# A hybrid decoder step on one Trainium2 core: seven products in the MLP's middle down projections, weight sums made by DMA, six raw weight buffers

## The chip, the cores and the metric

The kernel runs on one core of one Trainium2 chip. The metric is the device time of one execution in microseconds (us). The core's engines are PE (TensorE, matmuls), DVE (VectorE), ACT (ScalarE), POOL (GpSimd) and SP (SyncE, which here only issues DMAs). A matmul reads its operands from the on-chip memory SBUF and writes to PSUM; the inputs, the outputs and the weights lie in DRAM.

## The reference

One decoder layer in fp32 for 576 token columns: 512 prompt tokens and 64 sample tokens (8 sequences of 8). Cut to what matters here:

```python
m, s_gla_new, s_ret_new = mixer_block(rmsnorm(x, g_pre_mix), pos, s_gla, s_ret, w_in, ...)
x = x + rmsnorm(m, g_post_mix)
x = x + rmsnorm(cross_attn(rmsnorm(x, g_pre_xa), mem_k, mem_v, w_xq, w_xo), g_post_xa)
hf = rmsnorm(x, g_pre_ffn)
x = x + rmsnorm(jnp.square(jax.nn.relu(hf @ w_up)) @ w_down, g_post_ffn)
```

`mixer_block` projects to a gated linear attention branch and a retention branch of 4 heads each, with one state matrix a head, and merges them. `cross_attn` has 4 heads over 256 memory tokens; the prompt's keys and values are computed from `mem`, the samples' come from caches (`cache_mem_k`, `cache_mem_v`). `w_up` is 1024 x 4096 and `w_down` 4096 x 1024. The outputs are `y`, the new states and the prompt's new memory keys and values.

## The kernel before

Activations lie transposed: 1024 features as 8 blocks of 128 partitions, and 576 columns of tokens in two halves of 288 (`NH`). Every product is made from three matmuls in the reduced fp32r format: each operand is split into a high part (a cast on ACT, L93) and the rest (a subtraction on DVE, L94), and high x high, low x high and high x low are summed in PSUM (`mm3` L250, `gemm` L255). So a product of one 128x1024 weight tile with all columns is 8 x 3 x 2 = 48 matmuls of 128x288.

**Weights.** A list `plan` holds every weight tile in the order of its use. `wfetch` (L174) issues the next load on SP into one of `N_RAW` buffers `wraw` (4 of 128x1024 in the kernel before); `wsplit` (L183) casts the oldest into `wh` (ACT) and `wl` (DVE), three of each; `wnext` (L237) hands out a split tile and keeps `N_RAW - 1` loads asked for. The samples' cached keys and values (`in_ktc`, `in_vc`) go through the same `wraw` buffers in cross attention, and are used there without a split; how many stand after each weight tile is written in `KV_AFTER` (L31).

**Stages**, in order of time: the memory's keys and values (to about 62 us); the mixers, 8 units of one branch and one head each, `UNITS` (to about 565 us); the mix projection; cross attention, in two halves with `w_xq` and `w_xo`; the MLP. A tile scheduler sets each engine's order from the program; an engine takes its instructions in that order, and a DMA queue its loads.

**MLP.** Hidden features are taken in four groups of 1024, `g` = 0 to 3. Each group has an up stage (into `hh`, `hl`, after relu and square) and a down stage that adds to `y3`. Group 0's stages and all down stages are plain: 8 tiles of 48 matmuls. The up stages of groups 1 to 3 use `sevenfold` (L273): the weight is cut into 2x2 blocks, the activations into 2x2 (features by column halves), and the four result blocks come from seven products of block sums in place of eight. A call makes two blocks of 128 features, 7 x 12 = 84 matmuls; a stage is four calls. The sums of the activations are made once (`sums_f` L656, into `fsh`, `fsl`; "S1" to "S4" name the products of sums, "A11", "A12", "A22" those of plain blocks). The sums of the weights are made on DVE, four subtractions of 128x512 a call (`minus` L213, called by `begin` L203), from two tiles of `w_ups`.

**Mixers.** For each head, DVE and POOL make the norms of the output (`mv`, then `rs` on POOL, L874, then `on` on DVE, L878 and L880), POOL makes `ks` (L1063), masks `sm` (L965), the rotary products `t` (L890) and gates `G` (L1127); `s0` is a head's state, loaded by SP.

Of the kernel before, what the change touches and what calls it, by code (L numbers as in the profile page):

```python
# [22 lines left out]
N_RAW = 4  # L23
# [3 lines left out]


RING, STAY, RAW, SEVEN = 0, 1, 2, 3
# [29 lines left out]
def decoder_step(ctx, tc, xT, memT, ktc, vc, s_gla, s_ret, w_in, w_ga, w_a2, w_mix, w_xq, w_xk, w_xv, w_xo,  # L59
                 w_up, w_ups, w_down, vecs, cst, gam, y_out, mk_out, mv_out, sg_p, sr_p, sg_s, sr_s):  # L60
# [102 lines left out]
    def seven(w, b0):  # L163
        return [(w[b0 + b][:, kh], SEVEN) for b in range(4) for kh in range(2)]
# [6 lines left out]
    wq = []  # L171
    units = []

    def wfetch():  # L174
        if plan and sum(m == SEVEN for _, m in raws) < 2:
            src, mode = plan.pop(0), RING
            if isinstance(src, tuple):
                src, mode = src
            raw = wp.tile([P, 1024], F32, name="wraw", bufs=N_RAW)
            nc.sync.dma_start(out=raw if len(src.shape) == 2 else raw.rearrange("p (k n) -> p k n", n=src.shape[2]), in_=src)  # L180
            raws.append((raw, mode))

    def wsplit():  # L183
        if units:
            units.pop(0)()
        elif raws:
            if raws[0][1] == SEVEN:
                begin()
                return
# [4 lines left out]
            pool = staying[-1] if mode == STAY else wp  # L194
            wh = pool.tile([P, 1024], F32R, name="wh")
            wl = pool.tile([P, 1024], F32R, name="wl")
            split(wh, wl, raw)
            ready.append((wh, wl))

    def halves(w):  # L200
        return w.rearrange("p (q n) -> p q n", q=2)

    def begin():  # L203


        while len(raws) < 2:
            wfetch()
        p0, p1 = (raws.pop(0)[0] for _ in range(2))
        t = wp.tile([P, 1024], F32, name="wraw", bufs=N_RAW)
        q0, q1, qt = halves(p0), halves(p1), halves(t)  # L210

        def minus(out, a, b):
            nc.vector.tensor_tensor(out=out, in0=a, in1=b, op=ALU.subtract)  # L213

        def ring(raw):
            wh = wp.tile([P, 1024], F32R, name="wh")
            wl = wp.tile([P, 1024], F32R, name="wl")
            split(wh, wl, raw)
            ready.append((wh, wl))

        def own(raw, o, n):
            w = wq[0][:, o:o + n], wq[0][:, o + n:o + 2 * n]
            split(*w, raw)
            ready.append(w)

        def unit_a():
            ring(p0)
            wfetch()

        units.extend([unit_a, lambda: ring(t), lambda: own(p1, 0, 1024),  # L230
                      lambda: minus(q1[:, 0], q1[:, 0], qt[:, 0]), lambda: own(q1[:, 0], 2048, 512)])
        minus(qt[:, 1], q1[:, 1], q0[:, 1])
        minus(q0[:, 1], q0[:, 1], q0[:, 0])
        minus(qt[:, 0], q1[:, 1], q0[:, 1])
        wfetch()

    def wnext(n=P):  # L237

        while sum(len(r) == 2 for r in ready) < 2 and (raws or plan):
            while not units and plan and len(raws) + sum(len(r) == 1 for r in ready) < N_RAW - 1:  # L240
                n0 = len(raws)
                wfetch()
                if len(raws) == n0:
                    break
            if not raws and not units:
                break
# [24 lines left out]


    def sevenfold(x, p1, p5, u2, c11, c22, c12, c21):  # L273


# [9 lines left out]
        def more():  # L285
            if units:
                wsplit()

        while len(ready) < 3:
            wsplit()  # L290
        acc, b, c = atile()[:, :NH], otile()[:, :NH], gtile()[:, 0, :NH]
        wa, wc, wb = (ready.pop(0) for _ in range(3))
        prod(acc, wa, 0, "A11", True)
        p1(acc)
        while units:
            wsplit()
        wd = ready.pop(0)
        prod(c, wa, 1, "S1", True)
        p5(c)
        if raws and raws[0][1] == SEVEN:  # L300
            begin()
        prod(acc, wc, 0, "S2", False)
        wsplit()
        u2(acc)
        prod(b, wb, 0, "A12", True)
        more()
        c11(b)
        prod(acc, wc, 1, "S3", False)
        c22(acc)
        prod(c, wb, 1, "S4", False)  # L310
        c12(c)
        more()
        prod(acc, wd, 0, "A22", False)
        more()
        c21(acc)
# [332 lines left out]
    xnp = ctx.enter_context(tc.tile_pool(name="xnp", bufs=2))  # L648
# [4 lines left out]
    def add(out, a, b, op=ALU.add):  # L653
        nc.vector.tensor_tensor(out=out, in0=a, in1=b, op=op)  # L654

    def sums_f():  # L656

        for j in range(4):
# [5 lines left out]
            add(c2[:, 1], c2[:, 0], c2[:, 1])  # L664
            add(c2[:, 0], c1[:, 0], c2[:, 0], ALU.subtract)
            add(c1[:, 0], c2[:, 1], c1[:, 0], ALU.subtract)
            add(c1[:, 1], c1[:, 1], c1[:, 0], ALU.subtract)
            yield
            split(fsh[:, 2:4, j], fsl[:, 2:4, j], c2)
            split(fsh[:, 0:2, j], fsl[:, 0:2, j], c1)  # L670
            yield

    FQ = {"A11": (fh, fl, 0), "A12": (fh, fl, 1), "A22": (fh, fl, 3),
# [748 lines left out]
```

## Time and profile before

| | |
|---|---|
| median of 3 runs | 1206.34 us (1204.42 to 1206.52) |
| profiled execution, its own time | 1206.06 us |
| its span, first to last instruction | 1204.3 us |
| mean granted clock of PE | 0.988 of full speed |
| PE busy | 1172.6 us, 97% |
| DVE, ACT, POOL busy | 745.9, 564.3, 152.8 us |
| DMA | 158.37 MB, mean 131 GB/s |

The profiled execution took 1.8 us more than its span (start and end of the program) and 0.28 us less than the median. The engines are in step with PE almost everywhere, so what counts is the time in which PE does nothing, how many matmuls it has, and which of its two clock levels it is given. "x" in the rows counts instructions; a wait is put down to the one releaser that came last.

### The profile page before, as it was taken

To read this page: it belongs to the slowest core of one execution; us is meant where nothing else is said; L and a number is where in the kernel's file an instruction comes from. 1 tells how busy PE (TensorE), PEld (TensorE's weight loads), DVE (VectorE), ACT (ScalarE), POOL (GpSimd) and SP (SyncE) were. 2 spreads that over 40 slices of the span, in tenths; PEclk is the share of its full clock that TensorE was granted. 3 is DMA by queue.
4 is the path that set the end of the run, shared out by engine and by line. 5 is a ranking of instruction groups with operands and counts; after the bars stand their busy time and mean duration, and the time that the engine had idled before them with its cause. 6 is when DMAs were issued, how large, how long until landed. Compare 5 with 4: busy or idle time off the path is not lost.

```text
span 1204.3 us, 21958 instructions
## 1 busy us (share of the span) xinstructions
PE 1172.6 (97%) x9006; PEld 1140.8 (95%) x9006; DVE 745.9 (62%) x1332; ACT 564.3 (47%) x992; POOL 152.8 (13%) x165
## 2 busy tenths in 40 slices
PE   8999999999999999999999999999999999999995
PEld 7999999999999999999999877989999999999995
DVE  6756556565756575658677544686847457555665
ACT  6624455533544344434565444556437316415652
POOL 0621213131312231221001000000000000000000
PEclk9999999999999999999999999999999999999998
DMA  7852324242324242422644676654322322422641
GB/s 268 277 195 90 125 70 130 79 136 80 127 80 127 88 128 71 142 75 91 213 150 138 232 252 233 196 160 127 105 71 87 107 70 65 129 71 70 199 145 60
DMA packets 65621, 158.37 MB, mean 131 GB/s; under 512 B 5648, under 2 KB 34448, under 8 KB 65392
## 3 DMA queue, kind: packets, MB, share of 16 engines
q1 hardware_dynamic: 65520, 156.96, 40.9%
q8 instruction: 71, 1.16, 0.4%
q14 instruction: 30, 0.25, 0.1%
HBM read 140.68 MB, written 16.25 MB: 130 GB/s over the span
## 4 chain that ended last, share of the span: by engine, by line
PE 86%; DVE 6%; DMA 3%; ACT 3%; issue 1%; POOL 1%; SPq 0%; POOLq 0%; DVEq 0%; ACTq 0%
PE psg L252 23%; PE psg L251 23%; PE psg L253 23%; PE psa L281 4%; PE psg L281 2%; PE psa L251 1%; DVE wl L94 1%; PE psa L252 1%; PE psa L253 1%; PE pso L281 1%; DMA wraw<-in_w_xo 1%; PE pso L1241 1%; DMA wraw<-in_w_down 1%; PE psa L1084 1%; ACT wh L93 1%; DVE res L526 1%
## 5 line engine op out<-in xcount | busy, mean ns | idle before, releaser
L251 PE MATMUL psg<-xh,wh 128*128 128x288 f32 x1296 | 386.6, 298 | 3.2 <-ACT wh L93 3.2
L252 PE MATMUL psg<-xh,wl 128*128 128x288 f32 x1296 | 383.6, 296 | 2.5 <-DVE wl L94 2.5
L253 PE MATMUL psg<-xl,wh 128*128 128x288 f32 x1296 | 383.1, 296 | 0.0
L94 DVE TENSOR_TENSOR wl<-wraw,wh 128x1024 fp32r<-128x1024 f32 x197 | 243.8, 1238 | 89.9 <-ACT wh L93 88.9
L93 ACT CAST wh<-wraw 128x1024 fp32r<-128x1024 f32 x197 | 206.9, 1051 | 164.5 <-PE psg L253 104.6
L251 PEld LDWEIGHTS psg<-xh,wh 128*128 128x128 f32 x1296 | 244.3, 189 | 5.5 <-ACT wh L93 4.1
L252 PEld LDWEIGHTS psg<-xh,wl 128*128 128x128 f32 x1296 | 244.6, 189 | 3.3 <-DVE wl L94 3.2
L253 PEld LDWEIGHTS psg<-xl,wh 128*128 128x128 f32 x1296 | 244.4, 189 | 0.1
L251 PE MATMUL psg<-hh,wh 128*128 128x288 f32 x512 | 151.9, 297 | 0.7 <-DVE y L760 0.6
L252 PE MATMUL psg<-hh,wl 128*128 128x288 f32 x512 | 150.7, 295 | 0.3 <-DVE wl L94 0.3
L253 PE MATMUL psg<-hl,wh 128*128 128x288 f32 x512 | 150.7, 295 | 0.0
L251 PEld LDWEIGHTS psg<-hh,wh 128*128 128x128 f32 x512 | 96.1, 188 | 1.6 <-issue 1.1
L252 PEld LDWEIGHTS psg<-hh,wl 128*128 128x128 f32 x512 | 96.1, 188 | 0.6 <-DVE wl L94 0.6
L253 PEld LDWEIGHTS psg<-hl,wh 128*128 128x128 f32 x512 | 96.1, 188 | 0.0
L333 POOL TENSOR_TENSOR rs<-ms,mhalf 96x3 f32<-96x3 f32 (+1 forms) x11 | 11.0, 1000 | 527.4 <-DVE ms L326 527.4
L942 ACT COPY vt<-psg 128x512 f32<-128x512 f32 x16 | 9.4, 586 | 78.2 <-PE psg L253 78.2
L874 POOL TENSOR_TENSOR rs<-mv,mhalf 128x1 f32<-128x1 f32 x48 | 29.8, 621 | 112.6 <-DVE mv L869 64.5
L654 DVE TENSOR_TENSOR y<-psg,y 128x576 f32<-128x576 f32 x16 | 12.1, 758 | 50.4 <-PE psg L253 50.4
L944 DVE COPY vd<-psg 128x128 f32<-128x128 f32 x32 | 7.8, 286 | 56.0 <-ACT vt L942 56.0
L251 PE MATMUL psg<-bh,wh 128*128 128x288 f32 x128 | 38.9, 304 | 1.6 <-ACT wh L93 1.1
L252 PE MATMUL psg<-fh,wl 128*128 128x288 f32 x128 | 38.8, 303 | 0.9 <-DVE wl L94 0.9
L251 PE MATMUL psg<-fh,wh 128*128 128x288 f32 x128 | 39.0, 305 | 0.3 <-ACT fh L93 0.2
(324 smaller groups left out, 2400.2 us busy)
## 6 DMA issues: line engine op xcount, KB each, us to landing
wraw<-in_w_in SPq DMA_DIRECT2D x64, 512.0 KB, 3.6
wraw<-in_w_down SPq DMA_DIRECT2D x38, 512.0 KB, 3.7
wraw<-in_w_ups SPq DMA_DIRECT2D x24, 512.0 KB, 3.7
wraw<-in_ktc SPq DMA_DIRECT2D x16, 512.0 KB, 4.4
wraw<-in_vc SPq DMA_DIRECT2D x16, 512.0 KB, 5.2
wraw<-in_w_xq SPq DMA_DIRECT2D x14, 512.0 KB, 4.5
wraw<-in_w_xo SPq DMA_DIRECT2D x14, 512.0 KB, 5.2
wraw<-in_w_up SPq DMA_DIRECT2D x14, 512.0 KB, 4.5
```

The costliest lines, as they stand in the source:

```text
L93: nc.scalar.copy(hi, src)
L94: nc.vector.tensor_tensor(out=lo, in0=src, in1=f32(hi), op=ALU.subtract)
L251: nc.tensor.matmul(out, ah, bh, start=first, stop=False)
L252: nc.tensor.matmul(out, al, bh, start=False, stop=False)
L253: nc.tensor.matmul(out, ah, bl, start=False, stop=last)
L281: nc.tensor.matmul(out, s[:, q, k], m[:, k], start=first and k == i == 0, stop=k == 3 and i == 2, skip_group_check=True)
L333: nc.gpsimd.tensor_tensor(out=rs[:t, :n], in0=ms, in1=mhalf[:t, :n], op=ALU.pow)
L526: nc.vector.tensor_tensor(out=res[:, kk, c], in0=y[:, kk], in1=rj, op=ALU.add)
L654: nc.vector.tensor_tensor(out=out, in0=a, in1=b, op=op)
L874: nc.gpsimd.tensor_tensor(out=rs[:t], in0=mv[:t], in1=mhalf[:t, 0:1], op=ALU.pow)
L1084: nc.tensor.matmul(U[:, j * 256:(j + 1) * 256], kst[g][:, 2 * bp + j, :], vst[g], start=True, stop=True)
L1241: nc.tensor.matmul(acc[rows, :256], x(h), w[:, h], start=first, stop=last, skip_group_check=True, tile_position=(0, 32 * h))
```

## The change

The diff does four things.

1. The down stages of groups 1 and 2 use `sevenfold` too (`xh7` gives it the blocks). For that, the up stages of these groups end by making the sums of their results (`pairs`, into `hh` and `hl`) beside the plain blocks (`ha`, and the third quarter of `fh`, `fl`). Group 3's stages keep their forms. `sevenfold` evicts its own products now, and with `late` it makes the product A12 second.
2. All weight sums, of 20 calls, are made in DRAM (`t_sev`) by DMAs that `sums()` issues during the mixers, four times a unit: for each pair of calls four copies on SP (L197 after) and four transfers on POOL that add to what lies there (L195 after). The DVE subtractions of weights go. A call then loads seven pieces of 256 KB in seven DMAs, in place of two tiles of 512 KB.
3. `N_RAW` is 6 instead of 4, for all weights and the cached keys and values.
4. The weights' buffers are filled by `wmore` inside `sevenfold`; the last, half-size tile of a call has its own buffer (`LAST`, pool `wdp`).

The core of it:

```diff
-N_RAW = 4
+N_RAW = 6
...
+SUMS_AT = (2, 4, 6, 8, 10, 12, 15, 17, 19, 21)
+SUM_STEPS = (0, 0, 2, 2, 4, 6, 8, 10)
...
+    def seven(b0):
+        out = []
+        for n in range(b0, b0 + 4):
+            g, i = n // 2, n % 2
+            b = [w_sev[q, n] for q in range(4)]
+            t1, t2, t4 = t_sev[g]
+            out += [((b[0], t1[i]), RING), ((t2[0, i], t2[1, i]), RING), ((b[2], b[3]), RING), ((t4[i],), LAST)]
+        return out
...
-        plan += seven(w_ups, 4 * (g - 1))
-        plan += whole(w_down, 4 * g) + (rest(whole(w_down, 12), 0) if g == 3 else [])
+        plan += seven(8 * (g - 1))
+        plan += seven(8 * g - 4) if g < 3 else whole(w_down, 4) + rest(whole(w_down, 4), 0)
...
+    steps = {}
+    for g, at in enumerate(SUMS_AT):
+        b11, b12, b21, b22 = (w_sev[q, 2 * g:2 * g + 2] for q in range(4))
+        t1, t2, t4 = t_sev[g]
+        for n, (dst, src, plus) in zip(SUM_STEPS, (
+                (t1, b11, 0), (t2[1], b12, 0), (t1, b12, 1), (t2[1], b22, 1),
+                (t2[0], t1, 0), (t2[0], b22, 1), (t4, t2[0], 0), (t4, b21, 1))):
+            steps.setdefault(at + n, []).append((dst, src, plus))
+    clock = [0]
+
+    def sums():
+        for dst, src, plus in steps.pop(clock[0], ()):
+            if plus:
+                nc.gpsimd.dma_start(out=dst, in_=src, accum_op=ALU.add, max_dma_last_dim=8192)
+            else:
+                nc.sync.dma_start(out=dst, in_=src)
+        clock[0] += 1
...
         prod(acc, wa, 0, "A11", True)
-        p1(acc)
-        while units:
-            wsplit()
+        nc.scalar.copy(c1[:, 0], acc)
+        if late:
+            c11()
+        prod(c, wa, 1, "S1", True)
+        nc.scalar.copy(c2[:, 1], c)
+        wmore()
         wd = ready.pop(0)
...
+    def pairs(c1, c2, sh, sl):
+        add(c2[:, 1], c2[:, 0], c2[:, 1], ALU.subtract)
+        add(c2[:, 0], c1[:, 0], c2[:, 0], ALU.subtract)
+        split(sh[:, 2:4], sl[:, 2:4], c2)
+        add(c1[:, 0], c2[:, 1], c1[:, 0], ALU.subtract)
+        add(c1[:, 1], c1[:, 1], c1[:, 0])
+        split(sh[:, 0:2], sl[:, 0:2], c1)
...
+            def done1():
+                relu2(c1)
+                split(*((hh[:, 0:2, b], hl[:, 0:2, b]) if plain else (ha[:, 0, :, b], ha[:, 1, :, b])), c1)
+
+            def done21(ps):
+                relu2(c2[:, 0], ps)
+                if plain:
+                    split(hh[:, 2:4, b], hl[:, 2:4, b], c2)
+                else:
+                    pairs(c1, c2, hh[:, :, b], hl[:, :, b])
...
+        for b in range(4):
+            c1, c2 = (hp.tile([P, 2, NH], F32, name="hr") for _ in range(2))
+            y = [y3[:, 2 * b:2 * b + 2, hc(half)] for half in range(2)]
...
+            sevenfold(xh7, c1, c2, lambda: add(y[0], y[0], c1), lambda: None, done21, b == 0)
```

**Where the order of instructions moves.** Numbers behind names count buffers; "waits" names the counters that an instruction waits for (`PE_49` is PE's, `DMASW` those of POOL's transfers, `DMAHW` those of SP's).

SP in cross attention's first half, before: cached values (`in_vc`) between the tiles of `w_xq`.

```order
L180 DMA wraw_8576<-in_vc 128x1024 [waits DMAHW1_49,PE_49]
L180 DMA wraw_8607<-in_w_xq 128x1024 [waits DMAHW3_49,DVE_49]
L180 DMA wraw_8613<-in_vc 128x1024 [waits DMAHW4_49,PE_49]
L180 DMA wraw_8634<-in_vc 128x1024 [waits DMAHW7_49,DVE_49]
L180 DMA wraw_8655<-in_vc 128x1024 [waits DMAHW5_49,PE_49]
L180 DMA wraw_8687<-in_w_xq 128x1024 [waits DMAHW6_49,PE_49]
```

And with the change, at the same place:

```order
L213 DMA wraw_8654<-in_vc 128x1024 [waits DMAHW2_49,DVE_49]
L213 DMA wraw_8656<-in_vc 128x1024 [waits DMAHW7_49,PE_49]
L213 DMA wraw_8658<-in_w_xq 128x1024 [waits DMAHW3_49,DVE_49]
L213 DMA wraw_8660<-in_vc 128x1024 [waits DMAHW0_49,PE_49]
L213 DMA wraw_8691<-in_vc 128x1024 [waits DMAHW1_49,PE_49]
L213 DMA wraw_8697<-in_vc 128x1024 [waits DMAHW7_49,DVE_49]
L213 DMA wraw_8718<-in_w_xq 128x1024 [waits DMAHW4_49,PE_49]
```

The last row is the same `w_xq` tile in both. Before, its buffer is that of the fourth load ahead of it, and the load just ahead of it takes the buffer of the first row shown. With the change its buffer is that of the sixth load ahead of it, the first row shown.

PE where the up stage of group 1 hands over to its down stage, with the change (`ha` holds the plain blocks of the up stage's result, `hh` the sums; `psa`, `pso`, `psg` are the products A11, A12 and S1):

```order
L276 MATMUL pso_11464<-ha_10886,wh_11435 128x288 x2
L276 MATMUL pso_11464<-ha_10886,wl_11436 128x288
L276 MATMUL pso_11464<-ha_10886,wh_11435 128x288
L276 MATMUL psa_11463<-ha_10886,wh_11374 128x288 [waits Activation_49]
L276 MATMUL psa_11463<-ha_10886,wl_11375 128x288
L276 MATMUL pso_11464<-ha_10886,wh_11435 128x288
L276 MATMUL pso_11464<-ha_10886,wl_11436 128x288
L276 MATMUL psg_11465<-hh_10884,wh_11374 128x288
L276 MATMUL psg_11465<-hh_10884,wl_11375 128x288
L276 MATMUL psg_11465<-hl_10885,wh_11374 128x288
L276 MATMUL psg_11465<-hh_10884,wh_11374 128x288
L276 MATMUL psa_11463<-ha_10886,wh_11374 128x288 [waits DVE_49]
```

Products of plain blocks (`ha`) of the down stage stand ahead of and between those of sums (`hh`, `hl`); before, the down stage is plain, and there are no products of sums.

POOL in the mixers' third unit, before (`ql`, `ks` operands of the heads, `sm` masks):

```order
L98 TENSOR_TENSOR ql_2573<-qf_2571,qh_2572 128x512 [waits Activation_49]
L965 AFFINE_SELECT sm_2795<-sm_2795 128x128 [waits Activation_49]
L1063 TENSOR_TENSOR ks_2826<-klo_2821,cm_828 128x512 [waits DVE_49]
L965 AFFINE_SELECT sm_2860<-sm_2860 128x128 [waits Activation_49,Pool_49]
L1063 TENSOR_TENSOR ks_2890<-klo_2885,cm_828 128x512 [waits DVE_49,PE_49]
L965 AFFINE_SELECT sm_2952<-sm_2952 128x128 [waits Activation_49,Pool_49]
```

And with the change, with transfers that add into `t_sev` (its number is the pair of calls and the piece):

```order
L101 TENSOR_TENSOR ql_2588<-qf_2586,qh_2587 128x512 [waits Activation_49]
L195 DMA t_sev30<-in_w_sev 64x2048 [waits DMAHW6_49,DMASW0_49]
L986 AFFINE_SELECT sm_2816<-sm_2816 128x128 [waits Activation_49]
L1084 TENSOR_TENSOR ks_2847<-klo_2842,cm_832 128x512 [waits DVE_49]
L195 DMA t_sev31<-in_w_sev 64x2048 [waits DMAHW7_49,DMASW1_49]
L986 AFFINE_SELECT sm_2881<-sm_2881 128x128 [waits Activation_49,Pool_49]
L1084 TENSOR_TENSOR ks_2911<-klo_2906,cm_832 128x512 [waits DVE_49,PE_49]
L986 AFFINE_SELECT sm_2973<-sm_2973 128x128 [waits Activation_49]
```

Two transfers now stand between the operations, each behind a copy on SP; in all there are 40, and nine of them stand directly ahead of an `rs` operation.

SP in the same unit, with the change:

```order
L1097 DMA s0_2991<-in_s_gla 128x4x256 [waits DMAHW4_49,PE_49]
L197 DMA t_sev02<-t_sev01 16x8192 [waits DMAHW5_49,DMASW4_49]
L1116 DMA out_sgs<-sn_3000 128x2x256 [waits DMAHW6_49,DVE_49,Activation_49]
L1116 DMA out_sgs<-sn_3083 128x2x256 [waits DMAHW7_49,DVE_49,Activation_49]
L197 DMA t_sev21<-t_sev20 16x8192 [waits DMAHW0_49,DMASW5_49]
L197 DMA t_sev40<-in_w_sev 16x8192 [waits DMAHW1_49]
L197 DMA t_sev41<-in_w_sev 16x8192 [waits DMAHW2_49]
L213 DMA wraw_3095<-in_w_in 128x1024 [waits DMAHW3_49]
L1097 DMA s0_3158<-in_s_gla 128x4x256 [waits DMAHW4_49,PE_49]
```

The second state load (`s0`) stands behind four copies of 512 KB and two stores of states; before, there are no copies.

## Rows read from the trace of the kernel before

**Rows 1.** The page's list of busy engines: us, share of span, instructions.

```profile
PE 1172.6 (97%) x9006; PEld 1140.8 (95%) x9006; DVE 745.9 (62%) x1332; ACT 564.3 (47%) x992; POOL 152.8 (13%) x165
```

**Rows 2.** Busy time by stretches: mixers, cross attention, its half clock, up stage of group 1.

```profile
core 0: us, PE busy (x) PEld busy (x) DVE busy (x) ACT busy (x) POOL busy (x), PEclk, DMA share, GB/s
...
60.00:545.00 485.00, 484.25 (x3782) 475.09 (x3782) 295.80 (x669) 210.06 (x418) 110.00 (x113) 1.00 0.35 109
...
680.00:760.00 80.00, 73.82 (x626) 63.35 (x625) 33.52 (x59) 31.64 (x64) 3.07 (x6) 0.96 0.70 229
...
695.00:700.00 5.00, 5.00 (x35) 4.60 (x38) 1.14 (x1) 1.05 (x1) 0.00 (x0) 0.72 0.61 228
...
896.00:942.00 46.00, 45.56 (x340) 45.09 (x339) 31.41 (x42) 29.71 (x50) 0.00 (x0) 1.00 0.34 106
```

**Rows 3.** Waits of PE in the whole run: us, times, longest.

```profile
PE psg L252 <- DVE wl L94: 5.2, 8, 0.9
...
PE psg L251 <- ACT wh L93: 4.2, 3, 1.6
...
PE psa L281 <- ACT hr L726: 1.0, 3, 0.4
...
PE psa L956 <- ACT T L995: 0.8, 1, 0.8
```

**Rows 4.** Waits of PE from 680 to 760 us (cross attention).

```profile
PE psg L251 <- ACT wh L93: 3.2, 2, 1.6
...
PE psg L252 <- DVE wl L94: 1.7, 2, 0.9
```

**Rows 5.** The chain of waits from 684 us: start, us, what.

```profile
685.90 6.36 DMA wraw<-in_w_xq
...
694.69 0.61 PE psg L252
...
697.70 0.24 PE psg L251
```

**Rows 6.** The chain of waits in the up stage of group 1.

```profile
898.45 1.60 PE psg L281 x12
```

**Rows 7.** SP's timeline from 683 us: start, us, instruction.

```profile
682.99 2.82 SPq L180 DMA_DIRECT2D wraw<-in_vc  x3
```

**Rows 8.** ACT's groups by shape, 885 to 932 us (three sevenfold calls).

```profile
L93 ACT CAST wh<-wraw 128x1024 fp32r<-128x1024 f32 x9 | 9.5, 1055 | 2.5 <-DMA wraw<-in_w_down 2.2
...
L93 ACT CAST hh<-hr 128x576 fp32r<-128x576 f32 x4 | 2.5, 666 | 0.0
...
L717 ACT ACTIVATE hr<-hr 128x576 f32<-128x576 f32 x3 | 2.0, 683 | 0.4 <-DVE hr L654 0.4
...
L713 ACT ACTIVATE hr<-hr 128x288 f32<-128x288 f32 x3 | 1.3, 443 | 5.4 <-DVE hr L654 5.4
```

**Rows 9.** DVE's groups by shape in the same stretch.

```profile
L94 DVE TENSOR_TENSOR wl<-wraw,wh 128x1024 fp32r<-128x1024 f32 x9 | 11.0, 1224 | 15.2 <-ACT wh L93 15.2
...
L213 DVE TENSOR_TENSOR wraw<-wraw 128x512 f32<-128x512 f32 x11 | 7.6, 691 | 0.3
...
L94 DVE TENSOR_TENSOR hl<-hr,hh 128x576 fp32r<-128x576 f32 x4 | 2.8, 752 | 0.0
...
L654 DVE TENSOR_TENSOR hr<-pso,hr 128x288 f32<-128x288 f32 x3 | 1.4, 453 | 0.6 <-PE pso L281 0.6
```

**Rows 10.** POOL's groups by shape, whole run.

```profile
L1127 POOL TENSOR_TENSOR G<-G,t 128x576 f32<-128x576 f32 x14 | 20.2, 1440 | 20.0 <-ACT t L1126 20.0
...
L890 POOL TENSOR_TENSOR t<-t,t 128x576 f32<-128x576 f32 x8 | 19.2, 2398 | 35.4 <-DVE t L889 35.4
...
L1063 POOL TENSOR_TENSOR ks<-klo,cm 128x512 fp32r<-128x512 f32 x16 | 16.7, 1042 | 84.2 <-DVE klo L1040 84.2
...
L965 POOL TENSOR_SCALAR_AFFINE_SELECT sm<-sm 128x128 f32<-128x128 f32 x16 | 4.8, 298 | 95.0 <-ACT sm L964 95.0
```

**Rows 11.** Waits of DVE from 60 to 562 us.

```profile
DVE on L880 <- POOL rs L874: 13.2, 24, 0.7
```

More of the change, by code (lines that the diff above doesn't have):

```diff
@@ L170, in decoder_step @@
+    clock = [0]
[6 more added lines that the diff above has]
+        clock[0] += 1
     raws, ready, staying = [], [], []
-    wq = []
-    units = []
+    wdp = []
     def wfetch():
-        if plan and sum(m == SEVEN for _, m in raws) < 2:
+        if plan:
             src, mode = plan.pop(0), RING
-            if isinstance(src, tuple):
+            if isinstance(src, tuple) and isinstance(src[1], int):
@@ L193, in wsplit, with wmore @@
                 return
[L194 to L197, printed above, removed]
+            n = 512 if mode == LAST else 1024
+            pool = wdp[0] if mode == LAST else staying[-1] if mode == STAY else wp
+            wh = pool.tile([P, n], F32R, name="wh")
+            wl = pool.tile([P, n], F32R, name="wl")
+            split(wh, wl, raw[:, :n])
             ready.append((wh, wl))
[L200 to L206, printed above, removed]
+    def wmore():
+        while plan and len(raws) < N_RAW - 1:
             wfetch()
[L208 to L235, printed above, removed]
+        wsplit()
     def wnext(n=P):
         while sum(len(r) == 2 for r in ready) < 2 and (raws or plan):
-            while not units and plan and len(raws) + sum(len(r) == 1 for r in ready) < N_RAW - 1:
-                n0 = len(raws)
+            while plan and len(raws) + sum(len(r) == 1 for r in ready) < N_RAW - 1:
                 wfetch()
-                if len(raws) == n0:
-                    break
-            if not raws and not units:
+            if not raws:
                 break
@@ L663, in sums_f @@
             yield
[L664 to L667, printed above, removed]
+            pairs(c1, c2, fsh[:, :, j], fsl[:, :, j])
             yield
[L669 to L673, printed above, removed]
-          "S2": (fsh, fsl, 0), "S4": (fsh, fsl, 1), "S3": (fsh, fsl, 2), "S1": (fsh, fsl, 3)}
+    SQ = {"S2": 0, "S4": 1, "S3": 2, "S1": 3}
     def xf7(n):
-        h, l, q = FQ[n]
-        return h[:, q], l[:, q]
+        return (fsh[:, SQ[n]], fsl[:, SQ[n]]) if n in SQ else tuple(
+            t[:, {"A11": 0, "A12": 1, "A22": 3}[n]] for t in (fh, fl))
     y3 = None
@@ L683, in decoder_step, with xh7 @@
         hl = acta.tile([P, 4, 4, NH], F32R, name="hl", tag="xl")
+        plain = g in (0, 3)
+        ha = None if plain else biga.tile([P, 2, 2, 4, NH], F32R, name="ha", tag="biga")
+        def xh7(n):
+            if n in SQ:
+                return hh[:, SQ[n]], hl[:, SQ[n]]
+            return (fh[:, 2], fl[:, 2]) if n == "A22" else (ha[:, 0, n == "A12"], ha[:, 1, n == "A12"])
         if g == 0:
@@ L703, in decoder_step @@
                     lows.pop(0)()
+            xns.close()
+            wdp.append(ctx.enter_context(tc.tile_pool(name="wdp", bufs=1)))
             y3 = bigb.tile([P, KT, NT], F32, name="y3", tag="res")
             side.append(sums_f())
[L706 to L727 removed]
@@ L739, in decoder_step, with done21 @@
+        if plain:
+            break
+        for b in range(4):
+            c1, c2 = (hp.tile([P, 2, NH], F32, name="hr") for _ in range(2))
+            y = [y3[:, 2 * b:2 * b + 2, hc(half)] for half in range(2)]
+            def done21(ps):
+                nc.scalar.copy(c2[:, 0], ps)
+                add(y[1], y[1], c2)
+            sevenfold(xh7, c1, c2, lambda: add(y[0], y[0], c1), lambda: None, done21, b == 0)
     res2 = fsp.tile([P, KT, NT], F32, name="res2", tag="fsh")
@@ L1122, in unit @@
                 tick()
+            sums()
             for m in range(2):
@@ L1128, in unit @@
                 tick()
+            sums()
             def finish():
```

119 lines of the change are left out of this document (53 added, 66 removed).

## The prediction

> **What bounds the kernel now.** I read the page's list of busy engines first. PE is busy for 1172.6 us of the 1204.3 us span, 97% [rows 1]; the next engine, DVE, is at 62%. So the only large thing that a change can buy is fewer matmuls, and the only other thing is the 32 us in which PE stands still, and what it then loses at half its clock.
>
> The table by stretches [rows 2] says where that is. From 60 to 545 us (the mixers) PE is busy for 484.25 of 485 us. From 680 to 760 us (cross attention) it is busy for 73.82 of 80, at a mean granted clock of 0.96. In the up stage of the MLP's group 1, the first by seven products (896 to 942 us), it is busy for 45.56 of 46.
>
> PE's waits [rows 3] then name what it waited for. In the whole run the weights' casts cost it 5.2 + 4.2 = 9.4 us, the last values of an up stage (`hr` of L726) 1.0 us in three waits, and the mixers one wait of 0.8 us. In cross attention alone [rows 4] the casts cost 3.2 + 1.7 = 4.9 us, two waits on each of ACT and DVE, so two stalls of 2.45 us.
>
> The chain of waits shows what is behind the first of them [rows 5]: the load of a `w_xq` tile was issued at 685.90 us and took 6.36 us, then cast and remainder, and then 12 single matmuls from 694.69 to 697.94 us (the first and the last stand there), against 1.60 us for 12 in the MLP, 0.133 each [rows 6]. The granted clock from 695 to 700 us was 0.72 [rows 2]: after the idle stretch the chip gave the lower of its two levels (1.2 GHz) for a while. SP's row [rows 7] shows three cached value tiles going out at 682.99 us and ending at 685.81, just before that load: the `w_xq` load stood behind them in SP's order.
>
> **The change, part by part.**
>
> *The products.* Two down groups drop from 8 x 48 = 384 to 4 x 84 = 336 matmuls, together 96 fewer. At 1.60/12 = 0.133 us [rows 6] that is **-12.8 us**, and all of it is on the path, as PE is.
>
> *The two stalls of cross attention.* With four raw buffers the late `w_xq` tile takes the slot of the tile four places back, behind another load that waits for PE. With six it takes that of the sixth back, a value tile that PE has read by 682.99 us, when the loads that now reuse it go out [rows 7]: 2.9 us before 685.90, with fewer transfers ahead of it. A stall is 2.45 us, so that covers it. Each stall also cost the half clock, 3.25 us for 12 matmuls in place of 1.60, so 1.65. Together 2 x (2.45 + 1.65): **-8.2 us**. If the loads are bound by the memory (229 GB/s from 680 to 760 us [rows 2]) more buffers don't help, and this term is 0. The other 4.5 us of casts that PE waits for lie elsewhere; I leave them, and half of them, 2.3 us, go into the range's lower end.
>
> *DVE's sums of weights.* 48 instructions of 0.691 us [rows 9], 33 us, go from DVE. They stand beside matmuls: 0.
>
> *The up stages of groups 1 and 2.* Here work is added: the eight calls now also make the sums of the activations. Per call, ACT has three casts of 1.055, one of at most 0.666, eight operations on 288 columns of 0.443, two on 576 of 0.683 and three casts of 576 of 0.666 [rows 8]; with every one in sequence 3.2 + 0.7 + 3.5 + 1.4 + 2.0 = 10.8 us. DVE has three remainders of 1.224, four of 0.752, and eight operations on 288 columns of 0.453 [rows 9]: 10.3 us. A call's 84 matmuls take 84 x 0.133 = 11.2 us. So both fit, with 0.4 and 0.9 us to spare: **0**. If they don't, a call waits for one cast, 1.055, and eight of them cost 8.4 us.
>
> *Handing over.* Where an up stage ends, PE waits for the last `hr` values, 1.0 us in three waits now [rows 3]. Five stages now begin or end with products by sums. In two of them the chain behind the last product is longer by two subtractions (2 x 0.453) and a split (0.666 [rows 8] + 0.752 [rows 9]), 2.3 us in all; but the change's order runs A11 and A12 of the down stage first, which need only the older values, and these are 2 x 1.60 us of cover. So I take 0.3 us for each of the five, the size of one of the three waits: **+1.5 us**. The bounds are 0 and 2 x 2.3 + 3 x 1.0 = 7.6.
>
> *The mixers.* They get 40 copies (SP) and 40 accumulating transfers (POOL) of 512 KB. That is 80 x 0.524 MB = 42 MB in 485 us, 86 GB/s on top of 109 at a DMA share of 0.35 [rows 2]; in proportion the share becomes 0.63, or 0.91 if each byte is moved twice. From 680 to 760 us the share was 0.70 at 229 GB/s, so there is room for the first; weights are asked for several tiles of 48 x 0.133 = 6.4 us ahead. On SP, a state load now stands behind up to four copies: 5 x 0.524/229 = 11.4 us, while its reader comes some 270 matmuls, 36 us, later. Both 0.
>
> POOL is the open one, because no accumulating transfer is in the trace of before. From below, POOL's short `sm` operation is 0.30 us; from above, its long `t` operation 2.40 [rows 10]. I take 1.04, that of `ks`, a value between the two: the accumulate hands a transfer on and computes nothing, but names many more pieces than a copy of one tile. Nine of the 40 stand directly ahead of an `rs` operation, for which DVE then waits (24 waits of at most 0.7 us at one such line [rows 11]): 9.4 us on DVE. DVE is busy for 295.8 of 485 us [rows 2], and PE had one wait in the mixers [rows 3]; a fifth of it reaching PE is **+2 us**. The bounds are 0 and 40 x 2.40 = 96.
>
> By the Trainium skill (SBUF — State Buffer, "SBUF: two separate sides") a transfer that POOL issues has its descriptors written by GpSimd, which is locked out while DVE runs certain two-port operations; it tells of one that took about 3100 ns in place of 620. That speaks against this change, since DVE is busy for 61% of the mixers; the trace of before has no transfer from POOL in them, but POOL's own 128x576 operations read 1.44 us at one line and 2.40 at another [rows 10]. By the Trainium skill's two figures 40 x 2.5 = 100 us could be lost, if PE waited for every one.
>
> For the transfers the Trainium skill (Collectives: The Full Stack, "The bandwidth ceiling: the fold count and why AG ≠ RS ≠ AR") says that adding in the DMA needs two source reads, so about half the rate; by it the share of 0.91 above holds rather than 0.63. No run here shows it yet.
>
> **The sum.** The profiled execution took 1206.06 us; the median is 1206.34, 0.28 more. 1206.06 - 12.8 - 8.2 + 1.5 + 2 = 1188.6, and at the median's level **1188.8 us**, 17.5 us (1.5%) faster. A measurement of this kernel can tell about 0.2%, 2.4 us, from no change.
>
> **The rivals.**
> *Six buffers give nothing* because cross attention is bound by its transfers. For it: the load took 6.36 us where 229 GB/s would give 2.3. Against it: it started late, behind PE's use of a slot. 1188.8 + 8.2 = 1197.0. Chance 0.12.
>
> *ACT or DVE bound the up stages.* For it: 10.8 of 11.2 us is close, and casts wait for a free `wh`. Against it: the durations of neighbours overlap in the trace. 1188.8 + 8.4 = 1197.2. Chance 0.12.
>
> *Late weights or states in the mixers* through SP's longer queue or a DMA share of 0.91: the 11.4 us above at most, 1190 to 1200. Chance 0.05.
>
> *Slower: the accumulates hold POOL, POOL holds DVE at `on`, and PE waits.* In the place of one wait of 0.8 us the mixers would have up to 40. It decides from (17.5 + 2)/40 = 0.49 us that reach PE per accumulate. At POOL's shortest operation, 0.30, and one mean DVE operation of the mixers that it waits out (295.8/669 = 0.44), each is 0.74: without the 2 us above, 1186.8 + 40 x 0.74 = 1216. At 1.0 each it is 1227. For it: POOL feeds DVE in every head, and 24 waits already stand there. Against: PE felt none of those, and only nine accumulates stand ahead of an `rs`. Chance 0.13. The rule of the Trainium skill (SBUF — State Buffer) above is this mechanism, and gives more.
>
> *The gains just cancel* (accumulates at 0.43 to 0.55 us): within 0.2%. Chance 0.03. That the change doesn't do what it says has no room: the 96 matmuls and the 48 sums are gone from the engines' orders.
>
> **The numbers.** The forecast, 1183 to 1193, has 0.55. Its lower end is 1188.8 - 1.5 - 2 - 2.3 = 1183.0; with the three cases to 1203 the range of **1183 to 1203** holds about 0.82. Faster 0.55 + 0.12 + 0.12 + 0.05 = 0.84, same 0.03, slower 0.13.
>
> **What would show it.** PE's busy time should fall by about 13 us, with 96 fewer matmuls. The two idle stretches of cross attention and the half clock behind them should be gone, and with them `psg` waits on `wh` and `wl`. In the up stages of groups 1 and 2 PE should wait for no `wh` or `wl`, with ACT near 0.95. In the mixers PE should still be busy for over 99%; waits of PE that follow `on` <- `rs`, or a POOL that is busy far over 110 us, would mean that the slower rival holds. The forecast is wrong if cross attention keeps its stalls, or if the mixers end more than 5 us later than now.

## The result, and the profile after

The change takes 1277.97 us (median of 4 runs, 1276.83 to 1278.33); the kernel before took 1206.43 us beside it. The ratio is 1.060, 95% interval 1.058 to 1.062: the change is 71.5 us slower. The forecast was 17.5 us faster.

The page of the change, its first lines, its clock by fortieths of the span, and the queue of POOL's transfers (packets, MB, share of 16 engines):

```profile
span 1276.6 us, 22259 instructions
...
PE 1194.2 (94%) x8910; PEld 1149.6 (90%) x8910; DVE 760.8 (60%) x1372; ACT 597.9 (47%) x1070; POOL 177.7 (14%) x205
...
PEclk9899999999997897998999999999999999999998
...
q0 software_dynamic: 3200, 20.97, 9.0%
```

Against [rows 1] PE has 96 instructions fewer, as it should, and is busy for longer, since matmuls at the lower clock are longer. The clock row has its low digits in the first half, which is the mixers. The first PE instructions that read the normed tokens (`xh`), the merged mixers (`bh`) and the MLP's input (`fh`), and the last that reads the hidden values (`hh`), cut the two traces into the same stages:

| us | start | mixers | mix projection and cross attention | MLP | rest |
|---|---|---|---|---|---|
| before | 62.4 | 504.7 | 220.7 | 402.2 | 14.4 |
| change | 67.7 | 591.0 | 216.6 | 386.6 | 14.6 |
| difference | +5.3 | +86.3 | -4.1 | -15.6 | +0.2 |

So the gain is there, where it was looked for, and the mixers lose five times as much. The mixers as a whole, first before, then with the change (the columns are those of [rows 2]):

```profile
62.36:567.06 504.70, 503.95 (x3938) 494.22 (x3937) 311.01 (x710) 219.38 (x437) 114.04 (x118) 1.00 0.34 107
```

```profile
67.69:658.66 590.97, 539.02 (x3938) 515.54 (x3937) 311.67 (x709) 221.98 (x439) 136.85 (x158) 0.95 0.56 164
```

PE has the same 3938 matmuls in both. With the change it stands still for 52.0 us of the stage, before for 0.8, and it is busy for 35.1 us longer at a mean clock of 0.95 in place of 1.00. These two make up the 86.3 us. Two stretches of the mixers with the change, and two of the MLP (group 1's up and down stages):

```profile
core 0: us, PE busy (x) PEld busy (x) DVE busy (x) ACT busy (x) POOL busy (x), PEclk, DMA share, GB/s
...
370.00:430.00 60.00, 45.90 (x293) 43.17 (x291) 20.95 (x49) 17.13 (x38) 12.92 (x18) 0.85 0.44 117
430.00:490.00 60.00, 45.34 (x294) 40.77 (x295) 32.50 (x84) 17.92 (x43) 12.96 (x17) 0.81 0.65 196
```

```profile
983.00:1028.00 45.00, 45.00 (x339) 45.00 (x338) 34.12 (x52) 34.36 (x63) 0.00 (x0) 1.00 0.46 148
1028.00:1073.00 45.00, 45.00 (x335) 44.47 (x334) 29.99 (x43) 23.10 (x38) 0.00 (x0) 1.00 0.51 163
```

In the first of them PE runs 293 matmuls in 60 us, where before it ran 470 to 472 in each 60 us from 130 to 550 us. The DMA engines are at 0.44 there and at 0.65 in the second, and DVE, ACT and POOL are busy for 54% of the time at most: no engine is full, each waits for others. In these stages of the MLP PE does not stop at all.

What PE waited for in the whole run (us, times, longest):

```profile
PE psg L247 <- DVE wl L97: 20.1, 16, 6.1
PE psg L246 <- ACT wh L96: 10.4, 7, 2.0
PE psa L1105 <- DVE on L897: 5.7, 4, 2.7
PE psg L246 <- DVE ga L828: 4.0, 1, 4.0
PE psa L1310 <- ACT osum L1306: 3.2, 1, 3.2
PE psa L323 <- DVE ss L321: 3.0, 1, 3.0
```

Against [rows 3] the casts of weights are late for 30.5 us (the first two rows), of which 23.7 lie in the mixers; the rest of PE's 52 us there is put down to other work of DVE and ACT, 12.1 of it to `on`. Why weights are late, SP's own waits from 60 to 600 us say (the DMA queue's, us, times, longest):

```profile
SPq L1116 <- DVE sn L1113: 194.0, 8, 62.1
SPq L213 <- DVE wl L97: 109.3, 16, 20.8
SPq L1116 <- DVE sn L1111: 78.8, 4, 31.7
```

L213 loads weights and waits for a free buffer, as it should. L1116 stores a sample state `sn`. SP stands at such stores for 273 us, once for 62.1; in the kernel before the same stores wait

```profile
SPq L1095 <- DVE sn L1090: 19.9, 4, 5.0
SPq L1095 <- DVE sn L1092: 15.6, 8, 2.4
```

and nowhere longer than 5.0. One of the longest in SP's timeline, and DVE's in the same stretch:

```profile
370.98 0.38 SPq L1097 DMA_DIRECT2D s<-in_s_gla  x1
372.21 0.48 SPq L197 DMA_DIRECT2D t_sev<-t_sev  x1
...
435.76 1.18 SPq L1116 DMA_DIRECT2D out_sgs<-sn  x2
436.99 0.49 SPq L213 DMA_DIRECT2D wraw<-in_w_in  x1
```

```profile
426.96 0.76 DVE L905 TENSOR_TENSOR t<-psg,cm 128x576 f32<-128x576 f32 x1 [13.15 <-PE psg L248]
...
431.84 2.35 DVE L97 TENSOR_TENSOR wl<-wraw,wh 128x1024 fp32r<-128x1024 f32 x2
434.11 1.28 DVE L1113 TENSOR_TENSOR sn<-s,psa 128x512 f32<-128x512 f32 x2
```

From 372.7 to 435.8 us SP issues nothing. It stands at the store of a state that DVE makes only at 434.1, because in DVE's order that stands behind rotary products (L905), which wait for PE, and behind the remainders of two more weight tiles (`wl`). These are the last tiles that SP had issued ahead of the store; the next ones stand on SP behind it. The state's load had gone out at 371. SP's order at this place, of the change (names count buffers as in the section on the change):

```
L213 DMA wraw_4406<-in_w_in 128x1024 [waits DMAHW0_49,Activation_49]
L213 DMA wraw_4539<-in_w_in 128x1024 [waits DMAHW1_49,DVE_49]
L1097 DMA s0_4617<-in_s_gla 128x4x256 [waits DMAHW2_49,PE_49]
L197 DMA t_sev42<-t_sev41 16x8192 [waits DMAHW3_49,DMASW3_49]
L1116 DMA out_sgs<-sn_4626 128x2x256 [waits DMAHW4_49,DVE_49,Activation_49]
L1116 DMA out_sgs<-sn_4709 128x2x256 [waits DMAHW5_49,DVE_49,Activation_49]
L213 DMA wraw_4717<-in_w_in 128x1024 [waits DMAHW6_49]
```

The orders give this a measure: the weight tiles that SP has ahead of a store, less those that DVE has split ahead of that state. It is what PE can still work from while SP stands; at the store shown above it is 0. Before it is 4 at all 32 stores, as many as there are buffers. With the change it is 3 to 6 in the first two of the eight units, 3 in the third, 1 in the fourth, 0, 0, 1 and 1 at the four stores of the fifth, 1 in the sixth, 2 in the seventh, and 3 to 6 in the last.

### The profile page after: what moved, and what is told of

The parts are those of the page before. It is cut to its first block, busy times and chain, and to the rows that moved or that the text cites. A ratio compares the mean times of both kernels' runs of the same rounds, so it can differ in the third digit from the quotient of the medians.

```text
span 1276.6 us, 22259 instructions
## 1 busy us (share of the span) xinstructions
PE 1194.2 (94%) x8910; PEld 1149.6 (90%) x8910; DVE 760.8 (60%) x1372; ACT 597.9 (47%) x1070; POOL 177.7 (14%) x205
## 4 chain that ended last, share of the span: by engine, by line
PE 56%; DVE 5%; issue 1%; POOL 1%; DMA 1%; ACT 1%; POOLq 0%; DVEq 0%; ACTq 0%
PE psg L247 11%; PE psg L248 10%; PE psg L246 10%; PE psa L276 10%; PE psg L276 5%; PE pso L276 3%; PE pso L1264 1%; PE psa L246 1%; DVE wl L97 1%; PE psa L248 1%; PE psa L247 1%; DVE res L525 1%; POOL rs L893 1%; DMA wraw<-in_w_xo 1%; PE psa L323 0%
## 5 line engine op out<-in xcount | busy, mean ns | idle before, releaser
L97 DVE TENSOR_TENSOR wl<-wraw,wh 128x1024 fp32r<-128x1024 f32 x237 | 281.9, 1192 | 146.1 <-ACT wh L96 141.1
L96 ACT CAST wh<-wraw 128x1024 fp32r<-128x1024 f32 x237 | 239.3, 1013 | 156.9 <-PE psg L248 63.8
L246 PE MATMUL psg<-hh,wh 128*128 128x288 f32 x256 | 75.8, 296 | 0.7 <-DVE y L779 0.6
L247 PE MATMUL psg<-hh,wl 128*128 128x288 f32 x256 | 75.6, 296 | 0.3 <-DVE wl L97 0.3
L248 PE MATMUL psg<-hl,wh 128*128 128x288 f32 x256 | 75.5, 296 | 0.0
L246 PEld LDWEIGHTS psg<-hh,wh 128*128 128x128 f32 x256 | 48.0, 188 | 1.2 <-issue 1.1
L247 PEld LDWEIGHTS psg<-hh,wl 128*128 128x128 f32 x256 | 48.1, 188 | 0.6 <-DVE wl L97 0.6
L248 PEld LDWEIGHTS psg<-hl,wh 128*128 128x128 f32 x256 | 48.0, 188 | 0.2 <-DVE hl L97 0.2
L247 PE MATMUL psg<-bh,wl 128*128 128x288 f32 x128 | 38.6, 302 | 3.5 <-DVE wl L97 3.5
L248 PE MATMUL psg<-fl,wh 128*128 128x288 f32 x128 | 37.9, 296 | 0.6 <-DVE fl L97 0.6
```

Of the source, the lines that this page charges most:

```text
L96: nc.scalar.copy(hi, src)
L97: nc.vector.tensor_tensor(out=lo, in0=src, in1=f32(hi), op=ALU.subtract)
L246: nc.tensor.matmul(out, ah, bh, start=first, stop=False)
L247: nc.tensor.matmul(out, al, bh, start=False, stop=False)
L248: nc.tensor.matmul(out, ah, bl, start=False, stop=last)
```

## The experiments

Three theories stood for the 86 us. **Order**: the engines' orders, which the scheduler writes from its own estimate of durations, are bad in the mixers. **POOL**: the slower rival of the prediction, by which the transfers hold POOL, and POOL holds DVE. **Memory**: the 42 MB that the sums move make loads late. All times are medians, beside the kernel before at 1205 to 1206 us.

### Without the transfers

```diff
-            t1, t2, t4 = t_sev[g]
+            t1, t2, t4 = w_sev[1, 2 * g:2 * g + 2], w_sev[2:4, 2 * g:2 * g + 2], w_sev[0, 2 * g:2 * g + 2]
...
-            steps.setdefault(at + n, []).append((dst, src, plus))
+            pass
```

> Leaves out: all 80 transfers that make the weights' sums; the seven-product calls load plain blocks in their place, so the products are not the reference's. Everything else is as in the change. SP-order theory (the 40 copies in SP's queue push the state loads and stores late, and SP stands at a store with the weights' loads behind it): mixers back from 591 to about 505 us, total 1188 to 1195 us. POOL theory (the accumulates hold POOL and so DVE): the same. Memory theory (42 MB more in the mixers make the weights' loads late): the same. It prices the rest of the change: if it stays above 1200 us, six buffers or the down stages cost time, and none of the three holds.

Measured 1188.93 us, ratio 0.986 (0.984 to 0.988). The mixers are at 504.7 us again. What is left of the change is worth 17 us: start +5.2, cross attention -6.1, MLP -15.5.

### One half of the transfers each

```diff
-            steps.setdefault(at + n, []).append((dst, src, plus))
+            if plus:
+                steps.setdefault(at + n, []).append((dst, src, plus))
...
-                nc.gpsimd.dma_start(out=dst, in_=src, accum_op=ALU.add, max_dma_last_dim=8192)
+                nc.gpsimd.dma_start(out=dst, in_=src, max_dma_last_dim=8192)
```

> Leaves out: the 40 copies on SP; the 40 transfers on POOL write plainly and add nothing, so the sums are not made. SP-order theory: 1188 to 1197 us, since SP has no copies. POOL theory: 1260 us or more, since POOL still issues all its 40 transfers. Memory theory: about half of the 86 us remains, some 1235 us.

Measured 1202.11 us, outside all three figures. The mixers take 505.5 us, but this does not speak against POOL: nothing holds these transfers any more, and the scheduler put six of them at 1.3 to 4 us and all of them into the first 152. They cost 11.7 us at the start, where the DMA share was 0.82 before and is 0.92 now. With `if not plus` in place of `if plus`:

> Leaves out: the 40 accumulating transfers on POOL; the 40 copies on SP stay, so the sums are not made. SP-order theory: 1265 to 1280 us, nearly all of the loss stays. POOL theory: 1188 to 1195 us. Memory theory: some 1235 us.

Measured 1280.59 us. The copies alone cost all of it (mixers 592.2 us), with no transfer on POOL. The POOL theory falls here. PE's waits for `on`, which the prediction had named as that rival's sign, are there all the same: 13.2 us in the mixers of this run, 12.1 in those of the change, the largest of them

```profile
PE psa L1106 <- DVE on L898: 5.9, 4, 2.7
```

### The copies issued by another engine

```diff
-                nc.sync.dma_start(out=dst, in_=src)
+                nc.gpsimd.dma_start(out=dst, in_=src)
```

> Computes all; the 40 copies are issued by POOL in place of SP, so POOL issues 80 transfers. SP-order theory: 1190 to 1200 us, SP's order has no copies. POOL theory: as slow as the change or slower, 1275 to 1330 us. Memory theory: the same traffic, so as the change, about 1278 us.

Measured 1275.28 us, near the figure of the memory theory. For the order theory this was a miss: SP's order had no copies, the measure was 6 at every store, and the mixers took 575.3 us still (the start was 11 us longer than in the change). With `nc.scalar` in place of `nc.gpsimd`:

> Computes all; the 40 copies are issued by ACT in place of SP, with the same 80 transfers in the mixers. In the engines' orders the new states (sn) stand within one weight tile of where they stood before, and SP has six weight tiles or more ahead of each store of a state. Order theory (the loss comes from engines' orders that put states late and SP's stores ahead of weights): 1190 to 1205 us. Memory theory (the copies' traffic holds the weights' loads): about 1275 us, as with the copies on SP or POOL.

Measured 1258.72 us, mixers 563.7: a miss again, and a point for memory as these expectations had put it. But the loss had other places. With the copies on POOL, DVE's states stand up to five weight tiles later than before in the fifth to seventh unit, so that order had only gone from SP. With them on ACT, POOL waits at its accumulates for the copies (us, times, longest, 130 to 640 us):

```profile
POOL t_sev L195 <- DMA t_sev<-in_w_sev: 30.0, 7, 5.9
```

and work stands behind them in order. Both runs left order and memory entangled. Their loss is not the one at SP's stores, since the measure is 6 or more at all stores of both. With the copies on POOL, PE's largest wait in the mixers is for a rotary product of DVE's and not for weights (us, times, longest):

```profile
PE psg L246 <- DVE t L908: 15.3, 4, 5.8
```

Why these two runs lose 71 and 59 us in the mixers stays open.

### The copies in the kernel before, and six buffers in the kernel before

The first has `sums()` and its four calls a unit, with `if not plus`, and nothing else of the change.

> The kernel before, with four raw buffers and its own down stages, and with only the 40 copies added on SP in the mixers (nothing reads them). Order theory: the stores stand zero to four weight tiles ahead in SP's order, as in the change, so the mixers lose 50 to 90 us: 1255 to 1295 us. If the loss needs six buffers or the transfers on POOL, it is 1206 to 1215 us.

Measured 1286.01 us, mixers 588.1 (+83.4); the measure is 0 to 4 at the stores. Neither six buffers nor the MLP has a part in the loss.

```diff
-N_RAW = 4
+N_RAW = 6
...
-    nc = bacc.Bacc("TRN2", target_bir_lowering=False, num_devices=1)
+    nc = bacc.Bacc("TRN2", target_bir_lowering=False, num_devices=1, dynamic_dma_scratch_size=4096)
```

> The kernel before with six raw buffers in place of four (and the smaller area for descriptors that makes room), nothing else. The two stalls of cross attention and their half clock go (8.2 us), and the first product behind the memory's keys and values comes some 5 us later, as in the change: 1202 to 1205 us. If six buffers give nothing in cross attention: 1209 to 1212 us.

Measured 1200.03 us, ratio 0.996 (0.995 to 0.998). Start +4.2 us, mix projection and cross attention -6.1, MLP -3.3. The MLP's part was not foreseen, so the time is 2 us under the range.

### The start

```diff
+    room = [3]
...
-            while plan and len(raws) + sum(len(r) == 1 for r in ready) < N_RAW - 1:
+            while plan and len(raws) + sum(len(r) == 1 for r in ready) < room[0]:
...
+    room[0] = N_RAW - 1
     mixers(tc, locals())
```

> Leaves out: the 80 transfers, as the run without sums (plain blocks are loaded in their place). Beside that, only three tiles are asked for ahead until the mixers begin, as with four buffers. If the late start comes from the two more weight loads ahead of the activations' loads, it starts as before and takes 5 us less than the run without sums: 1183 to 1185 us. If not, 1189 us.

Measured 1186.24 us, 2.7 less than the run without sums, between the two figures. In the trace the start is 5.2 us shorter, 62.4 us as before, and cross attention 1.5; the mixers are 1.1 us longer and the MLP 1.4.

### The same copies with shorter rows

The scheduler's estimate must hang on the copies' form, since the same bytes on POOL, in rows of 8 KB, moved nothing. A copy of 512 KB had been cut into 16 rows of 32 KB:

```diff
-                nc.sync.dma_start(out=dst, in_=src)
+                nc.sync.dma_start(out=dst, in_=src, max_dma_last_dim=4096)
```

> Computes all, as the change, on the same queues, in the same program order and with the same bytes; the 40 copies are only cut into 128 rows of 4 KB instead of 16 of 32 KB. That alone gives the engines' orders of before back: every new state (sn) stands at the same weight tile as before, and SP has six weight tiles ahead at each store. Order theory: the scheduler's estimate of the 16-row copies moved the order, and the time is that of the run without sums plus little, 1188 to 1196 us. Memory theory (traffic, or copies and accumulates waiting for each other in queues): 1255 to 1280 us.

And with `max_dma_last_dim=16384`:

> Computes all; as the run with 4 KB rows, but 32 rows of 16 KB, half the change's length. The order is nearly that of before (five to six weight tiles ahead at each store). Order theory: 1188 to 1200 us. If long pieces hold the transfer engines on the chip and the order is not it, the loss should be near the change's: 1235 to 1275 us.

Measured 1245.18 us with 4 KB, and **1192.44 us** with 16 KB, ratio 0.989 (0.987 to 0.991): faster than before by 13.4 us. The second is what the order theory says; the first is outside the figures of both theories, though the measure is 6 at every store. Two stretches of the mixers, first with 16 KB, then with 4 KB (same columns as in the stretches above):

```profile
130.00:190.00 60.00, 60.00 (x468) 59.31 (x468) 35.31 (x82) 30.21 (x59) 16.23 (x22) 1.00 0.80 211
190.00:250.00 60.00, 60.00 (x471) 58.81 (x470) 35.98 (x84) 32.30 (x65) 19.09 (x22) 1.00 0.81 226
```

```profile
130.00:190.00 60.00, 41.18 (x286) 39.31 (x285) 21.24 (x49) 16.30 (x26) 15.42 (x19) 0.81 1.03 289
190.00:250.00 60.00, 40.49 (x284) 37.74 (x283) 23.28 (x62) 19.26 (x46) 16.66 (x24) 0.81 1.00 289
```

With 16 KB rows the transfers run at a share of 0.80 and PE does not stop. With 4 KB rows the DMA engines are full. A second move of the scheduler's is behind that: the transfers on POOL end at 454 us with 16 KB rows, at 281 with 4 KB, and at 637 in the change. The bytes for each unit of share are much the same (289/1.03 and 211/0.80, 281 and 264 GB/s), so by this measure the short rows took no more of the engines' time for each byte; the transfers were packed into half the time. That the packing alone makes the loss is argued from these rows: no run has the 4 KB rows in the order of the 16 KB run. The chain of waits shows what was late then:

```profile
169.68 22.80 DMA t_sev<-t_sev
192.55 22.02 DMA t_sev<-t_sev
...
230.92 14.13 DMA out_sgs<-sn
```

From 310 us on, with all sums made, PE is at 60.00 of 60 in that run. Rows of 8 KB were to place the point:

> Computes all; the copies cut into 64 rows of 8 KB, the order nearly that of before. If only 4 KB pieces make the transfer engines run full, 1190 to 1200 us; if the copies' cost grows evenly as rows get shorter, between the runs with 16 KB and 4 KB rows, 1205 to 1230 us.

Measured 1214.90 us, mixers 533.1: between the two, with its last transfer on POOL at 298 us and the DMA share at 0.90 to 1.00 until 310. This is the time that the second figure gave; it does not tell the rows' length from the packing, since both changed. With the start of before, 4 KB rows:

> Computes all; the run with 4 KB rows and, until the mixers begin, only three weight tiles asked for ahead. Order theory: 2 to 5 us under the run with 4 KB rows, 1184 to 1193 us, under both kernels. Memory theory: 1250 to 1275 us.

Measured 1241.41 us: 3.8 less than without it, and still slower than before, so the expectation's figure missed with that of the run it rests on.

### The order pinned

The row length still changes two things, the order and the pieces that the chip moves. Here the program is built twice; the first build, with one row length, gives each engine's order, and the second, with the other, is tied to it one instruction behind the other.

```diff
+    ROWS[0] = ORDER_OF
+    first = build(None)
...
+    ROWS[0] = RUN_WITH
+    nc = build(order)
...
+            for names in order.values():
+                for a, b in zip(names, names[1:]):
+                    tc.add_manual_dep(at[b], a, ...)
```

> Computes all. The copies have 16 rows of 32 KB as in the change, but every engine's order is pinned to that of the run with 16 KB rows, instruction by instruction. Order theory: as that run, 1190 to 1197 us. If long pieces cost the time on the chip: 1260 to 1280 us.

> Computes all. The copies have 32 rows of 16 KB, but every engine's order is pinned to that of the change. Order theory: as the change, 1270 to 1285 us. If long pieces cost the time on the chip: 1190 to 1200 us.

In the traces each engine's instructions stand in the order of the run that they were tied to, with no difference in any of the five engines. Measured 1194.28 us for the change's own 32 KB pieces in the other order, and 1277.83 us for 16 KB pieces in the change's order. The mixers take 509.3 and 591.1 us. SP's waits at the same stores (60 to 600 us), first of the one, then of the other:

```profile
SPq L1118 <- DVE sn L1115: 38.8, 10, 11.2
```

```profile
SPq L1118 <- DVE sn L1115: 194.2, 8, 61.7
```

This settles what the change lost by. With the same instructions and bytes, the engines' order alone is worth 84 to 85 us, and the row length 0.1 to 1.8 us. The memory theory falls for the change: in a good order its 80 transfers cost the mixers 4 to 5 us. The pinned runs exchange the orders of all engines together; that within them the stores on SP hold the weights is read from SP's waits and the timeline above, and no run moves the stores alone.

### The best version

The run with 16 KB rows and the start of before:

> Computes all; the run with 16 KB rows and, until the mixers begin, only three weight tiles asked for ahead. The start comes back to that of before: 2 to 5 us under the run with 16 KB rows, 1187 to 1190.5 us. If the start costs nothing at the end (something else ends last): 1192 us.

Measured 1191.23 us, ratio 0.988 (0.986 to 0.990). The start is 3.7 us shorter in the trace, the mixers 1.6 longer; the median lies between the two figures, and the 1.2 us by which the medians differ are less than these runs can tell. Either version with 16 KB rows beats both kernels.

## Why the prediction was wrong

- **The products** were right: -12.8 us forecast. Six buffers alone bring the MLP from 402.2 to 398.9 us, the whole change to 386.6: 12.3 us for 96 matmuls (10.8 by the four runs whose MLP took 388.1 or 388.2).
- **The up stages** were right at 0. PE is busy for 45.00 of 45 us, ACT for 34.36 (76%; the sum of 10.8 of 11.2 us was an upper bound), and PE waits for no `wh` or `wl` in these stages.
- **Handing over** was +1.5 and came out at no cost: the three waits for `hr`, 1.0 us [rows 3], are gone, and the 12.3 us above hold whatever else it costs. The cover that was named, A11 and A12, was enough.
- **Cross attention** was -8.2; without sums it is -6.1, in the change -4.1. The two stalls went with their half clock, but a load of `w_xo`, issued at 784.01 us and 7.65 long in the chain, is late next and costs 3.2 us (`osum` above), with a clock of 0.93 from 775 to 800 us; in the change the mix projection also waits 3.5 us for its weights. Beyond that six buffers took 3.3 us out of the MLP, part of the range's lower end.
- **The start** was left out, and costs 5.3 us, also with six buffers alone (4.2): two more `w_xk` tiles go out ahead of the tokens, and PE waits 3.0 us for the statistics `ss`. With only three tiles asked for ahead it is 62.4 us again.
- **POOL** was priced at 1.04 us for one accumulate; the row says 0.866:

```profile
L195 POOL DMA_DIRECT2D t_sev<-in_w_sev x40 | 32.5, 866 | 9.2 <-DMA t_sev<-in_w_sev 9.0 <-issue 0.2
```

  In the change DVE's waits for `rs` at the line of [rows 11] are 9.8 us in 19 waits, at most 0.7, and so no more than before. With a good order all 80 transfers cost the mixers 4 us, where +2 was taken. Two signs of the slower rival did appear in the change, PE's waits for `on` (12.1 us) and a POOL busy for 136.9 us of the mixers in place of 114.0. The waits come without any transfer on POOL too, as the run with the copies alone shows.
- **The rival on the other side** had the right sign and the wrong place. Time was lost, but at SP's stores and not at POOL. The forecast had set the Trainium skill's rule on transfers from POOL (SBUF — State Buffer, "SBUF: two separate sides") beside that rival; the runs show no trace of it here: no accumulate held POOL for more than 1.4 us at its issue, and with 16 KB rows the mixers are 4.1 us longer with all 40 of them. The 61% that the forecast held against the change is all of DVE's busy time, and no row says how much of it is operations of the kind that the rule needs.
- **The DMA share** was worked out for the mixers as 0.63, or 0.91 if each byte moves twice. With 16 KB rows it is 0.68 over the mixers, and 0.80 while the sums run. What adding costs can be read from POOL's queue: plain, in the run without copies, and adding, in the run with 16 KB rows:

```profile
q0 software_dynamic: 3200, 20.97, 4.9%
```

```profile
q0 software_dynamic: 3200, 20.97, 10.2%
```

  4.9% of 1201.3 us and 10.2% of 1192.5 are 59 and 122 us for the same bytes, 2.1 times. The 40 copies on SP, of as many bytes, add 50 us to its queue in the kernel before (42.1% of 1288.1 us with them, 40.9% of 1204.3 without). So adding costs about twice and copying does not: 172 us in the 508.8 of the mixers, on top of the 0.34 of before, make the 0.68. The Trainium skill (Collectives: The Full Stack, "The bandwidth ceiling: the fold count and why AG ≠ RS ≠ AR") gives a reduction about half the rate of a copy, since it needs two source reads, and the 2.1 here agree.

**The step that failed** is the one on SP in the mixers: "On SP, a state load now stands behind up to four copies: 5 x 0.524/229 = 11.4 us, while its reader comes some 270 matmuls, 36 us, later. Both 0." The prediction had SP's order on the page, with the stores of states side by side and the second state load behind the copies, and priced the load. It did not price the stores: each is a wait on DVE with all later weights behind it, 273 us of SP's time in the change. Nor did it look at DVE's and PE's order in the mixers, by which a state came as much as 62.1 us after SP had reached its store. What was to be asked there is not how long a copy takes, but which weights are on the chip when SP begins to wait, and whether the work that ends the wait needs more than those. The rival "late weights or states", chance 0.05, named the queue but bounded it by the copies' own time, 11.4 us; it was 86.3. As the timeline reads, the wait feeds itself: PE starves, so the state comes later, so SP stands longer, and PE's clock falls to 0.81 to 0.85 in these stretches; the clock's part of the 86.3 is the 35.1 us of longer matmuls. That the run without the sums came out at the forecast time, 1188.93 us against 1188.8, is luck: 5.2 us of the start and 2.1 missing in cross attention were made up by 3.3 that six buffers gave in the MLP, by 1.5 of handing over that did not come, and by the 2 for POOL, which has no transfers in that run.

## What to carry to other kernels

Where a scheduler writes the orders, an added transfer is priced twice: by the chip and by the scheduler. After a change compare, at each wait in an in-order DMA queue, how many loads stand ahead of it with how many the waited-for work has used up by then; before, the difference was 4 everywhere, and it was 0 to 2 at the long waits. A full number is no promise: it was 6 or more in the runs with the copies on POOL or ACT and with 4 KB rows, which lost 58 to 71 us in the mixers all the same. If the number falls, look for a form of the added transfer that the scheduler prices nearer to the chip (here the row length), or pin the order, before giving up the idea.

## What the runs showed of the hardware that was not expected

Copies of 512 KB from DRAM to DRAM land in 7.0 us with 32 rows of 16 KB and 7.1 with 16 of 32 KB (the pinned run in the same order): between these two the piece length made no difference. At a DMA share of 0.80 and 211 to 226 GB/s the loads of weights still land in 4.8 us, against 3.6 before, and PE does not feel it; at 0.96 and more, 273 to 290 GB/s (rows of 4 and 8 KB), PE stops, and with 4 KB rows transfers in the chain take 14 to 23 us each. How densely these transfers may stand lies between the two.
